# A two-layer encoder on one Trainium2 core: a weight sum of the first chunk moved to an accumulating transfer, more weight quarters kept live, two squares moved to VectorE

## Chip, cores, metric

The kernel runs on one core of one Trainium2 chip. The metric is the device time of one launch in microseconds; lower is better. Every stated time is that of the one core.

## The reference, cut to what matters

Two encoder layers over 512 tokens of width 1024. Each layer normalises `x`, multiplies it by one wide input matrix, runs a token mixer (dilated windows in layer 0, grouped queries in layer 1) and an attention over 256 memory tokens, gates the result and adds an output projection.

```python
def reference(x, mem, norm_g, mem_norm_g, w_mem_kv, mem_qn_g, mem_kn_g, w_out,
              w_in_a, qn_a, kn_a, w_in_b, qn_b, kn_b):
    ...
    for i in range(DEPTH):                       # 2 layers
        h = rmsnorm(x, norm_g[i])
        mem_h = rmsnorm(mem, mem_norm_g[i])
        j = i // 2
        if i % 2 == 0:
            proj = jnp.einsum('bsd,de->bse', h, w_in_a[j])   # 512 x 1024 x 11264
            ...
            o_mix = mixer_dilated(qkv, qn_a[j], kn_a[j], ang_a)
        else:
            proj = jnp.einsum('bsd,de->bse', h, w_in_b[j])
            ...
        o_mem = memory_attention(q_mem, mem_h, w_mem_kv[i], mem_qn_g[i], mem_kn_g[i])
        y = jnp.concatenate([o_mix, o_mem], axis=-1) * jax.nn.silu(gate)
        x = x + jnp.einsum('bse,ed->bsd', y, w_out[i])
    return x
```

All data are float32. The kernel keeps that accuracy by splitting each operand into a rounded high part and a remainder and multiplying three times.

## The kernel before

**Chunks.** The weights are cut on the host into pieces of 128x1024 (512 KB), and the program consumes them in chunks (`PLAN`, in the order `SEQ = [1, 2, 0, 3, 4, ...]`). Chunks 1 and 2 (kind `T2`) are the keys and values of the memory tokens in layer 0: plain products. Chunk 0 (`W2`) makes the values `v0`, chunk 3 (`W1`) the memory queries, chunks 4 and on the heads. These use seven quarter products in place of eight (the scheme of Winograd): the weight matrix is cut into the quarters `11`, `12`, `21`, `22`, and four weight sums are formed from them:

- `T1` = quarter `12` with quarter `11` added (the host writes the signs so that all are additions),
- `T2` = quarter `22` plus `T1`, `T3` = quarter `12` plus quarter `22`, `T4` = quarter `21` plus `T2`.

The products run in the order `21, 11, T1, T2, 22, T3, T4`. In a chunk of kind `W2` each consists of two pieces (x = 0 and 1), in `W1` of one.

**Steps.** Each group of matmuls on TensorE takes one weight piece for all its tokens; after it the program calls `W.advance()` (L335), which raises the step number `g` by one. Steps 0 to 3 are the memory keys, 4 to 7 the memory values, 8 to 21 chunk 0 (two steps for each product in the order above: 8 and 9 take `21`, 10 and 11 `11`, 12 and 13 `T1`, 14 and 15 `T2`, 16 and 17 `22`, 18 and 19 `T3`, 20 and 21 `T4`), 22 to 28 chunk 3, 29 and on chunk 4. What one step puts into the program comes in this order:

1. `lo()` (L314): VectorE makes the low part `wo` = piece minus `wh` of pieces whose high part was made in an earlier step (line L319).
2. `sum()` (L265): at most one weight sum, the first in the list of those still to be made whose conditions hold. The list holds `T1, T2, T3, T4` (x = 0, then 1) of each chunk in turn. `T1` of chunks below 17 is an addition on VectorE (L278), the others are accumulating transfers issued by GpSimd (`G.dma_start(..., accum_op=ALU.add)`): `T2` and `T4` from another tile (L283, L293), `T3` from DRAM (L288). The conditions are counted in steps: a piece that was loaded at least `LEAD` = 2 steps earlier (`ripe`) may be added to, and `T1` also waits for step `T1_AT` = 8.
3. `hi()` (L300): ScalarE rounds up to two pieces into `wh` (L309), in the order of the products.
4. `dma()` (L251): SyncE loads further pieces while fewer than `KEEP[kind]` of them are live (10 for `W2`, 9 for `W1` and the first heads), at most nine in one step. A piece is live from its load to its last use.

Then the driver's `tick()` runs the other work of that step (norms, evacuations, attention) as generators. The schedule is written out in this way: every engine and every DMA queue runs its instructions in the order in which the program was written, and an instruction waits, on its engine, for the semaphores of what it needs.

**The work around the change.** `prep()` (L961) normalises `x` in four blocks c = 0 to 3: `norm_1` (L480) squares both halves on ScalarE (L488) and forms the root on GpSimd (L490, then `rstd_of`, L448 and L449), `norm_2` multiplies (L495, VectorE), `first_t` and `diffs_t` transpose the blocks and form the differences of the token quarters (L552 to L562), `rest_t` the rest (L569 to L575). `mem_kv` makes the memory keys: squares per head (L594), the root on GpSimd (L448, L449), a rescale on GpSimd (L658), the multiplication `xn` on VectorE (L599), and a transposition `qT` on TensorE (L606). In `s_chunk` (L376) a finished product is copied out of its PSUM bank by ScalarE (`keep`, L384) or added by VectorE (`add`, L401). Four PSUM banks (`pj`) go round, so a product with a fresh bank waits for the copies of the one before. `v0` is stored to DRAM by SyncE (L1062) as it is finished.

Of the kernel before, what the change touches and what calls it, by code (L numbers as in the profile page):

```python
# [21 lines left out]
TCKW = {}  # L22
NBIG, NM4, NS2, SCRATCH = 7, 23, 14, 2048
RING, LEAD = 4, 2
BULK, ACTIVE, SET_AT, T1_AT, MEM_B, PREP_Y, PREP_B, HALF, SET_B = 2, 2, 15, 8, 14, 1, 1, {"a": 3, "b": 3, "o": 0}, 9
MEM_STEP = 1, 1
MEM_D = 4
DIRECT, DIRECT_B = (7,), (4, 5, 6, 7)
# [9 lines left out]

SEQ = [1, 2, 0] + list(range(3, len(PLAN)))
T4_AT = {4: 4}  # L40
T1_DMA = 17
KEEP = {"T2": 8, "T2b": 6, "O1": 6, "W1": 9, "W2": 10, "W2s": 9, "W1bs": 9, "W1b": 7, "W2b": 9}


# [84 lines left out]
def trunk_kernel(ctx: ExitStack, tc: tile.TileContext, x, mem, wall, norm_g, mem_norm_g, gcol,  # L129
# [59 lines left out]
    def pieces(kind):  # L189

        return 2 * GROUPS[kind][0] if kind in GROUPS else 4 if kind in ("W1", "W1b", "W1bs") else 8

    class Weights:
        def __init__(self):
            self.items, self.last, self.need, self.allocs, self.sums = [], [], [], [], []
            self.users, self.kinds = {}, []
            g = 0
            for c in SEQ:
                kind, d = PLAN[c], sum(pieces(k) for k in PLAN[:c])
                base = len(self.items)  # L200
                if kind in GROUPS:
                    units, nb = GROUPS[kind]
                    if kind == "O1":
                        n = PLAN[c - 1] == "O1"
                        for x in range(2):
                            self.items.append((c, "P", x))
                            self.last.append(g + 5)
                            self.allocs.append(((c, "P", x), d + x, kind))
                            self.users[c, "P", x] = 1
                        self.need += [base + 2] * 2 if not n else [base + 2] * 6  # L210
                        g += 2 if not n else 6
                        units = 0
                    for u in range(units):
                        for x in (2 * u, 2 * u + 1):
                            self.items.append((c, "P", x))
                            self.last.append(g + (u + 1) * nb - 1)
                            self.allocs.append(((c, "P", x), d, kind))
                            self.users[c, "P", x] = 1
                            d += 1
                        self.need += [base + 2 * u + 2] * nb  # L220
                    g += units * nb
                else:
                    n = 1 if kind in ("W1", "W1b", "W1bs") else 2
                    at = {k: d + i * n for i, k in enumerate(("21", "11", "12", "22"))}
                    self.allocs += [((c, k, x), at[q] + x, kind) for k, q in LOADS for x in range(n)]
                    for k in ORDER:
                        for x in range(n):
                            self.items.append((c, k, x))
                            self.last.append(g)
                            self.need.append(len(self.items))  # L230
                            if k[0] == "T":
                                self.sums.append(((c, k, x), at["11" if k == "T1" else "22"] + x))
                            if k != "T4":
                                self.users[c, k, x] = 1 if k in ("22", "T3") or k == "11" and c >= T1_DMA else 2
                            g += 1
                self.kinds += [kind] * (g - len(self.kinds))
            assert sum(pieces(k) for k in PLAN) == wall.shape[0]
            self.g = -1
            self.live = 0
            self.tile, self.load_at, self.at, self.lo_at = {}, {}, {}, {}  # L240
            self.n_hi = self.n_lo = self.taken = 0
            self.op, self.hi_at = [], []
# [6 lines left out]
                self.live -= 1  # L249

        def dma(self, most=9):  # L251
            while self.allocs and self.live < KEEP[self.allocs[0][2]] and most:
                most -= 1
                key, d, _ = self.allocs.pop(0)
                self.live += 1
                self.tile[key] = m4(name="wl")
                self.load_at[key] = self.g
                if key[1][0] != "T":
                    self.at[key] = self.g
                nc.sync.dma_start(self.tile[key], wall[d])  # L260
# [4 lines left out]
        def sum(self, force=False, want=None):  # L265

            for n, (key, d) in enumerate(self.sums[:8]):
                if want and key != want:
                    continue
                c, k, x = key  # L270
                if k == "T1" and c >= T1_DMA:
                    if not self.ripe(self.load_at, key, force):
                        continue
                    G.dma_start(self.tile[key], wall[d], accum_op=ALU.add)
                elif k == "T1":
                    if not (self.ripe(self.load_at, key, force) and self.ripe(self.at, (c, "11", x), force)) or self.g < T1_AT and not force:
                        continue
                    V.tensor_tensor(self.tile[key], self.tile[key], self.tile[c, "11", x], ALU.add)  # L278
                    self.use((c, "11", x))
                elif k == "T2":  # L280
                    if not (self.ripe(self.load_at, key, force) and self.ripe(self.at, (c, "T1", x), force, 1 if c < T1_DMA else None)):
                        continue
                    G.dma_start(self.tile[key], self.tile[c, "T1", x], accum_op=ALU.add)  # L283
                    self.use((c, "T1", x))
                elif k == "T3":
                    if not self.ripe(self.load_at, key, force):
                        continue
                    G.dma_start(self.tile[key], wall[d], accum_op=ALU.add)  # L288
                else:
                    if not (self.ripe(self.lo_at, (c, "21", x), force, 1) and self.ripe(self.at, (c, "T2", x), force, T4_AT.get(c))):  # L290
                        continue
                    self.tile[key] = self.tile[c, "21", x]
                    G.dma_start(self.tile[key], self.tile[c, "T2", x], accum_op=ALU.add)  # L293
                    self.use((c, "T2", x))
                self.at[key] = self.g
                self.sums.pop(n)
                return True
            return False

        def hi(self, force=False):  # L300
            i = self.n_hi
            if i >= len(self.items) or not self.ripe(self.at, self.items[i], force, 1 if self.items[i][1] == "T1" and self.items[i][0] < T1_DMA else None):
                return False
            if i >= RING and self.last[i - RING] > self.g - (not force and self.items[i - RING][1] != "P"):
                return False
            self.n_hi += 1
            wh = pool.tile([128, 1024], F32R, tag="wh", name="wh", bufs=RING)
            wo = pool.tile([128, 1024], F32R, tag="wo", name="wo", bufs=RING)
            A.copy(wh, self.tile[self.items[i]])  # L309
            self.hi_at.append(self.g)  # L310
            self.op.append((wh, wo))
            return True
# [167 lines left out]
    def norm_1(xb, both=False):  # L480

        ss = sm(2, "ss")
        for j in range(2):
            jk = s2(name="sq")
            if both and j:
                V.tensor_tensor_reduce(jk, xb[j], xb[j], 1.0 / 1024.0, 0.0, ALU.mult, ALU.add, ss[:, j:j + 1])
            else:
                A.activation(jk, xb[j], AF.Square, scale=1.0 / 32.0, accum_out=ss[:, j:j + 1])  # L488
        r, e = sm(1, "rstd"), sm(1, "mse")
        G.tensor_tensor(e, ss[:, 0:1], ss[:, 1:2], ALU.add)  # L490
        return rstd_of(e, 1)
# [463 lines left out]
    xb = [halves(t) for t in xt]  # L955

    def prep():

        n = {}
        for c in range(5):  # L960
            if c < 4:  # L961
                n[c] = norm_1(xb[c])
            if c:
                norm_2(xb[c - 1], n[c - 1], rows["x"])
            if 1 < c < 4:
                first_t(H, xb[c - 2], c - 2)
            yield 1
        for c in range(2):
            yield from diffs_t(H, xb[2 + c], c)
            drv.spawn(rest_t(H, c, (2, 2, 2)), 1)  # L970
            yield 1
# [689 lines left out]
```

## Time and profile before

| | |
|---|---|
| time, median of 3 runs | 956.48 us (955.04 to 957.57) |
| the profiled execution, its own time | 955.29 us |
| its span (first to last instruction) | 953.4 us |
| TensorE busy in the span | 939.3 us (99%) |
| VectorE, ScalarE, GpSimd busy | 790.3, 680.8, 336.0 us |
| mean granted TensorE clock | 0.998 |

How to read the profile: PE is TensorE, PEld its weight loads, DVE is VectorE, ACT is ScalarE, POOL is GpSimd, SP is SyncE; a q behind the name stands for the engine's sequencer, which issues transfers. `L278` is line 278 of the kernel before. A row of the timeline has start, duration, engine, line, operation, output <- input, the number of instructions merged into the row, and in brackets how long the engine had been idle before and what ended that. In the rows on transfers, q1 is the queue of SyncE's loads and stores, q0 that of GpSimd's accumulating transfers; both share 16 DMA engines.

### The profile page before, as it was taken

The numbers are of one execution on the slowest core, as the hardware profiler recorded it, in microseconds if no ns is written. First come the engines' busy times: TensorE is split into PE (matmuls) and PEld (weight loads), VectorE is DVE, ScalarE is ACT, GpSimd is POOL, SyncE is SP. The second block draws the span as 40 slices with busy tenths as digits, with TensorE's granted clock in tenths as the row PEclk, the third lists the DMA queues.
The fourth block names the chain that finished last, engine by engine and source line by source line (L and its number), as shares of the span: only waits on it lengthen the run. The fifth ranks groups of instructions, "written<-read, shape, count | busy, mean of one in ns | idle before, by whom it ended". The sixth has DMA issues, their size and how long they took to land.

```text
span 953.4 us, 16569 instructions
## 1 busy us (share of the span) xinstructions
PE 939.3 (99%) x5680; PEld 832.2 (87%) x5680; DVE 790.3 (83%) x1409; ACT 680.8 (71%) x1700; POOL 336.0 (35%) x484
## 2 busy tenths in 40 slices
PE   8999999999999999999999999999899999999998
PEld 6878888888888888888889998888899999998886
DVE  6878776878888888979788999877988898779982
ACT  7773789686868686767775768547778877878860
POOL 3312423557454546463836111213232330111110
PEclk9999999999999999999999999999999999999999
DMA  9699966869787869696877989979966687786524
GB/s 352 271 217 337 335 156 177 289 123 265 148 259 157 264 155 265 155 257 142 229 182 197 259 200 252 288 251 314 240 158 132 192 236 174 210 210 178 123 59 129
DMA packets 86198, 203.51 MB, mean 213 GB/s; under 512 B 25057, under 2 KB 34529, under 8 KB 86114
## 3 DMA queue, kind: packets, MB, share of 16 engines
q1 hardware_dynamic: 66962, 139.46, 42.8%
q0 software_dynamic: 17856, 60.83, 34.4%
q10 hardware_dynamic: 1296, 2.16, 0.6%
q8 instruction: 45, 0.74, 0.3%
q14 instruction: 39, 0.32, 0.1%
HBM read 156.48 MB, written 11.34 MB: 176 GB/s over the span
## 4 chain that ended last, share of the span: by engine, by line
PE 84%; DMA 6%; DVE 5%; ACT 3%; issue 1%; SPq 1%; POOL 0%; DVEq 0%; POOLq 0%; ACTq 0%
PE pj L173 22%; PE pj L174 22%; PE pj L177 22%; PE qT L606 2%; DMA wl<-in_wall_dram 2%; DMA wl<-wl 2%; DVE wo L319 2%; PE sa L1181 1%; PE oo L1289 1%; PE pt L1268 1%; PE ptb L1491 1%; PE sa L1177 1%; DMA x<-in_x_dram 1%; DMA row<-in_norm_g_dram 1%; PE ob L177 1%
## 5 line engine op out<-in xcount | busy, mean ns | idle before, releaser
L319 DVE TENSOR_TENSOR wo<-wl,wh 128x1024 fp32r<-128x1024 f32 x255 | 312.3, 1231 | 5.3 <-ACT wh L309 5.1
L309 ACT CAST wh<-wl 128x1024 fp32r<-128x1024 f32 x255 | 268.5, 1060 | 42.9 <-PE pj L174 18.9
L173 PE MATMUL pj<-wh,hS 128*128 128x512 f32 (+1 forms) x448 | 158.0, 366 | 4.5 <-ACT sn L384 3.7
L174 PE MATMUL pj<-wh,hS 128*128 128x512 f32 (+1 forms) x448 | 152.6, 354 | 0.6 <-DVE hS L570 0.6
L173 PE MATMUL pj<-wh,h 128*128 128x512 f32 (+1 forms) x336 | 118.0, 365 | 0.3 <-DVE sn L401 0.3
L174 PE MATMUL pj<-wh,h 128*128 128x512 f32 (+1 forms) x336 | 114.2, 353 | 1.1 <-DVE h L570 1.1
L449 POOL TENSOR_TENSOR rstd<-mse,half 128x4 f32<-128x4 f32 (+2 forms) x96 | 101.7, 1059 | 8.0
L177 PE MATMUL pj<-wo,hS 128*128 128x512 f32 (+1 forms) x448 | 100.7, 354 | 0.0
L173 PEld LDWEIGHTS pj<-wh,hS 128*128 128x128 f32 x448 | 85.1, 190 | 15.4 <-ACT sn L384 4.3
L174 PEld LDWEIGHTS pj<-wh,hS 128*128 128x128 f32 x448 | 85.2, 190 | 11.1 <-DVE hS L570 0.8
L177 PEld LDWEIGHTS pj<-wo,hS 128*128 128x128 f32 x448 | 75.3, 191 | 12.0
L448 POOL TENSOR_SCALAR mse<-hss 128x4 f32<-128x4 f32 (+1 forms) x86 | 41.2, 479 | 117.6 <-ACT junk L594 113.2
L594 ACT ACTIVATE junk<-sn 128x128 f32<-128x128 f32 x264 | 79.1, 308 | 1.3 <-DVE sn L395 1.2
L1125 POOL TENSOR_TENSOR ta<-sn,tabs 128x128 f32<-128x128 f32 (+1 forms) x64 | 37.6, 595 | 117.8 <-DVE sn L599 91.2
L384 ACT COPY sn<-pj 128x512 f32<-128x512 f32 x116 | 64.5, 590 | 17.4 <-PE pj L177 16.6
L177 PE MATMUL pj<-wo,h 128*128 128x512 f32 (+1 forms) x336 | 74.9, 352 | 0.0
L174 PEld LDWEIGHTS pj<-wh,h 128*128 128x128 f32 x336 | 63.7, 190 | 8.8 <-DVE h L570 1.3
L173 PEld LDWEIGHTS pj<-wh,h 128*128 128x128 f32 x336 | 63.6, 189 | 8.0 <-DVE sn L401 0.7
L293 POOL DMA_DIRECT2D wl<-wl x33 | 30.3, 918 | 109.1 <-DVE wo L319 59.8
L401 DVE TENSOR_TENSOR sn<-pj,sn 128x512 f32<-128x512 f32 x87 | 59.5, 685 | 7.7 <-PE pj L177 7.3
L177 PEld LDWEIGHTS pj<-wo,h 128*128 128x128 f32 x336 | 56.0, 189 | 8.8
L283 POOL DMA_DIRECT2D wl<-wl x33 | 31.3, 974 | 77.8 <-DVE grA L984 19.3
(250 smaller groups left out, 2365.2 us busy)
## 6 DMA issues: line engine op xcount, KB each, us to landing
wl<-in_wall_dram SPq DMA_DIRECT2D x222, 512.0 KB, 7.4
wl<-wl POOLq DMA_DIRECT2D x66, 512.0 KB, 5.4
wl<-in_wall_dram POOLq DMA_DIRECT2D x42, 512.0 KB, 8.9
od<-o SPq DMA_DIRECT2D x11, 256.0 KB, 5.5
og<-od SPq DMA_DIRECT2D x10, 256.0 KB, 8.2
x<-in_x_dram SPq DMA_DIRECT2D x4, 512.0 KB, 9.0
v0d<-sn SPq DMA_DIRECT2D x8, 256.0 KB, 10.2
acc<-in_x_dram POOLq DMA_DIRECT2D x8, 256.0 KB, 7.3
```

Source lines behind the costliest of these rows:

```text
L173: T.matmul(o, a, b, start=start, stop=False, skip_group_check=True)
L174: T.matmul(o, c, d, start=False, stop=False, skip_group_check=True)
L177: T.matmul(o, a, b, start=False, stop=stop, skip_group_check=True)
L283: G.dma_start(self.tile[key], self.tile[c, "T1", x], accum_op=ALU.add)
L309: A.copy(wh, self.tile[self.items[i]])
L319: V.tensor_tensor(wo, self.tile[key], wh.bitcast(F32), ALU.subtract)
L384: A.copy(t, b)
L401: V.tensor_tensor(t, b, t, ALU.subtract if q == "12" else ALU.add)
L448: G.tensor_scalar(e, ss, EPS, None, ALU.add)
L449: G.tensor_tensor(r, e, half[:, 0:n], ALU.pow)
L594: A.activation(jk, p[:, j * 128:(j + 1) * 128], AF.Square, scale=by, accum_out=ss[:, j:j + 1])
L1125: G.tensor_tensor(ta[:, 0:n], xn[:, 0:n, 0:32], ropeA[:, 0, b, s0:s0 + n], ALU.mult)
```

## The change

In chunk 0 the sum `T1` is no longer an addition on VectorE: GpSimd issues an accumulating transfer that adds quarter `11` from DRAM, from step 7 on (`T1_AT` now holds for the transfers only). The tile of quarter `11` then has one user instead of two. `KEEP_C` raises the number of live pieces at which loading stops, to 14 while pieces of chunk 0 or 3 are next and to 12 for chunk 4. In `prep()`, the second square of blocks 2 and 3 is made by VectorE.

```diff
-BULK, ACTIVE, SET_AT, T1_AT, ... = 2, 2, 15, 8, ...
+BULK, ACTIVE, SET_AT, T1_AT, ... = 2, 2, 15, 7, ...
...
-T1_DMA = 17
+T1_DMA = 0, 17
+KEEP_C = {0: 14, 3: 14, 4: 12}
...
+    def by_dma(c):
+
+        return c == T1_DMA[0] or c >= T1_DMA[1]
...
-                                self.users[c, k, x] = 1 if k in ("22", "T3") or k == "11" and c >= T1_DMA else 2
+                                self.users[c, k, x] = 1 if k in ("22", "T3") or k == "11" and by_dma(c) else 2
...
         def dma(self, most=9):
-            while self.allocs and self.live < KEEP[self.allocs[0][2]] and most:
+            while self.allocs and self.live < KEEP_C.get(self.allocs[0][0][0], KEEP[self.allocs[0][2]]) and most:
...
-                if k == "T1" and c >= T1_DMA:
-                    if not self.ripe(self.load_at, key, force):
+                if k == "T1" and by_dma(c):
+                    if not self.ripe(self.load_at, key, force) or self.g < T1_AT and not force:
                         continue
                     G.dma_start(self.tile[key], wall[d], accum_op=ALU.add)
                 elif k == "T1":
-                    if not (self.ripe(self.load_at, key, force) and self.ripe(self.at, (c, "11", x), force)) or self.g < T1_AT and not force:
+                    if not (self.ripe(self.load_at, key, force) and self.ripe(self.at, (c, "11", x), force)):
                         continue
                     V.tensor_tensor(self.tile[key], self.tile[key], self.tile[c, "11", x], ALU.add)
...
                 elif k == "T2":
-                    if not (... self.ripe(self.at, (c, "T1", x), force, 1 if c < T1_DMA else None)):
+                    if not (... self.ripe(self.at, (c, "T1", x), force, 1 if c < T1_DMA[1] else None)):
...
         def hi(self, force=False):
-            if ... not self.ripe(self.at, self.items[i], force, 1 if self.items[i][1] == "T1" and self.items[i][0] < T1_DMA else None):
+            if ... not self.ripe(self.at, self.items[i], force, 1 if self.items[i][1] == "T1" and not by_dma(self.items[i][0]) else None):
...
-                n[c] = norm_1(xb[c])
+                n[c] = norm_1(xb[c], c > 1)
```

With its second argument set, `norm_1` (L480) makes the second square by `V.tensor_tensor_reduce`.

More of the change, by code (lines that the diff above doesn't have):

```diff
@@ L24 @@
 RING, LEAD = 4, 2
-BULK, ACTIVE, SET_AT, T1_AT, MEM_B, PREP_Y, PREP_B, HALF, SET_B = 2, 2, 15, 8, 14, 1, 1, {"a": 3, "b": 3, "o": 0}, 9
+BULK, ACTIVE, SET_AT, T1_AT, MEM_B, PREP_Y, PREP_B, HALF, SET_B = 2, 2, 15, 7, 14, 1, 1, {"a": 3, "b": 3, "o": 0}, 9
 MEM_STEP = 1, 1
@@ L280, in sum @@
                 elif k == "T2":
-                    if not (self.ripe(self.load_at, key, force) and self.ripe(self.at, (c, "T1", x), force, 1 if c < T1_DMA else None)):
+                    if not (self.ripe(self.load_at, key, force) and self.ripe(self.at, (c, "T1", x), force, 1 if c < T1_DMA[1] else None)):
                         continue
@@ L301, in hi @@
             i = self.n_hi
-            if i >= len(self.items) or not self.ripe(self.at, self.items[i], force, 1 if self.items[i][1] == "T1" and self.items[i][0] < T1_DMA else None):
+            if i >= len(self.items) or not self.ripe(self.at, self.items[i], force, 1 if self.items[i][1] == "T1" and not by_dma(self.items[i][0]) else None):
                 return False
```

## The prediction

> **What bounds the kernel now.** I read the page first, then the table of busy time by stretches, then TensorE's waits, then the timeline of the first 110 us. The first two rows say that TensorE is the bound: 14.1 us of the span are without a matmul, of which 7.25 us lie in the first 200 us, where the change acts.
>
> ```profile
> PE 939.3 (99%) x5680; PEld 832.2 (87%) x5680; DVE 790.3 (83%) x1409; ACT 680.8 (71%) x1700; POOL 336.0 (35%) x484
> 0.00:200.00 200.00, 192.75 (x1009) 162.80 (x1010) 154.04 (x221) 144.25 (x353) 71.79 (x114) 0.99 0.85 263
> PE pj L173 <- ACT sn L384: 3.7, 2, 1.9
> 50.97 0.50 PE L173 MATMUL pj<-wh,hS 128*128 128x512 f32 x1 [1.90 <-ACT sn L384]
> 96.83 0.38 PE L173 MATMUL pj<-wh,hS 128*128 128x256 f32 x1 [1.78 <-ACT sn L384]
> ```
>
> Two stalls stand out: 1.90 us ahead of step 12 (the first product with `T1`) and 1.78 us in chunk 3. The first costs more than its length, because the granted clock (third number from the end in these rows) falls behind it:
>
> ```profile
> 52.00:53.00 1.00, 1.00 (x5) 0.80 (x4) 0.97 (x3) 0.94 (x3) 1.00 (x2) 0.71 1.06 188
> 53.00:54.00 1.00, 1.00 (x4) 0.81 (x3) 1.00 (x2) 1.00 (x2) 0.06 (x1) 0.50 1.08 127
> 54.00:55.00 1.00, 1.00 (x3) 0.76 (x3) 1.00 (x3) 1.00 (x3) 0.00 (x0) 0.50 0.97 184
> 55.00:56.00 1.00, 1.00 (x4) 0.79 (x3) 1.00 (x2) 1.00 (x3) 0.53 (x1) 0.58 1.06 205
> ```
>
> 0.29 + 0.50 + 0.50 + 0.42 = 1.7 us of full-speed work are lost there. So the change can win at most about 1.9 + 1.7 + 1.78 = 5.4 us at these places.
>
> **Part 1: two additions leave VectorE.** VectorE works almost without a pause from 33.2 to 51 us, and step 12 waits for the end of that: differences (L561), a cast and a copy on ScalarE, then TensorE.
>
> ```profile
> 33.19 0.69 DVE L599 TENSOR_TENSOR xn<-pj,rstd 128x512 f32<-128x512 f32 x1 [0.51 <-POOL rstd L658]
> 44.18 1.22 DVE L278 TENSOR_TENSOR wl<-wl 128x1024 f32<-128x1024 f32 x1
> 47.96 1.22 DVE L278 TENSOR_TENSOR wl<-wl 128x1024 f32<-128x1024 f32 x1
> 49.09 0.68 DVE L561 TENSOR_TENSOR fS<-xT,f 128x512 f32<-128x512 f32 x1
> ```
>
> From the second addition to the next start are 49.09 - 47.96 = 1.13 us, so both are worth 2.26 us on this chain, more than the stall of 1.90.
>
> **Part 2: two squares.** Each leaves ScalarE (0.64 + 0.20 us) and goes to VectorE. The operation exists before only at another width:
>
> ```profile
> L488 ACT ACTIVATE sq<-x x8: 622/636/652, 18.4 to 29.8; 128x512 f32<-128x512 f32 x8
> L1187 DVE CUSTOM_DVE_ANT_0 p<-sa,tabs 128x256 f32<-128x256 f32 x48 | 19.0, 421 | 1.2 <-PE sa L1177 1.0
> ```
>
> At 512 wide it lies between 0.42 (the fixed part only) and 0.84 us (twice); I take 0.7. Both stand ahead of L599, where VectorE idles 0.51 us for GpSimd; with that cover gone the second costs up to 0.3 us. I count it at nothing, since part 3 makes that idle time much longer.
>
> **Part 3: more live pieces, and what they pull forward.** Counting pieces by the code's rules: before, chunk 0 loads four pieces by step 4 beyond the first six, and its last two (for `T3`) at steps 8 and 9. With 14 allowed (and nine loads at most in a step) the two `T3` pieces are loaded at step 2. `sum()` takes the first sum whose conditions hold. `T1` is held until step 7 and `T2` needs `T1`, but `T3` needs only its own load, two steps old. So the two `T3` transfers, at steps 12 and 13 before, now enter GpSimd's queue at steps 4 and 5. At step 4 `sum()` comes ahead of `tick()`, which issues the root for block 3 of `x` and the rescale of the memory keys (L658). Before, those ran straight on:
>
> ```profile
> 30.34 1.39 POOL L449 TENSOR_TENSOR rstd<-mse,half 128x4 f32<-128x4 f32 x1
> 31.68 0.20 POOL L490 TENSOR_TENSOR mse<-ss 128x1 f32<-128x1 f32 x1
> 32.83 0.33 POOL L658 TENSOR_SCALAR rstd<-rstd,rm 128x4 f32<-128x4 f32 x1
> 45.73 1.08 POOL L283 DMA_DIRECT2D wl<-wl  x1 [12.57 <-DVE wl L278]
> ```
>
> The first `T3` transfer will stand between the first two of these rows and wait there for its piece to land. That piece is the eleventh load of the weights after `x`, before and after: the first of these three issues.
>
> ```profile
> 29.12 2.87 SPq L260 DMA_DIRECT2D wl<-in_wall_dram  x3
> wl<-in_wall_dram SPq DMA_DIRECT2D x1, 512.0 KB, 10.2
> q1 hardware_dynamic: 228, 0.83, 103.7%
> q1 hardware_dynamic: 11, 0.03, 4.1%
> ```
>
> It landed at 29.1 + 10.2 = 39.3 us. An earlier issue doesn't bring it forward: the last two rows (36 to 38 us, 40 to 42 us) show the DMA engines full with such loads up to 38 us and empty after 40; they drain a queue whose order is unchanged. GpSimd does hold everything behind such a wait:
>
> ```profile
> 107.93 0.18 ACT L594 ACTIVATION_READ_ACCUMULATOR junk<-sn 128x1 f32 x1
> 108.80 0.92 POOL L293 DMA_DIRECT2D wl<-wl  x1 [3.42 <-DVE wo L319]
> 109.80 0.22 POOL L448 TENSOR_SCALAR mse<-hss 128x4 f32<-128x4 f32 x1
> ```
>
> The sum at 109.80 had its squares at 108.11 and began only after the transfer ahead of it was released and issued, 1.0 us after 108.80.
>
> So: 39.3 + 1.0 (issue) + 1.5 (31.68 to 33.16) = 41.8 us for the end of L658, against 33.2. `xn` (L599) runs 41.8 to 42.5, and TensorE, in order, stands at its transposition:
>
> ```profile
> 36.64 0.60 PE L606 MATMUL qT<-ident,xn 128*128 128x128 f32 x4
> 36.99 0.48 PE L173 MATMUL pj<-wh,h 128*128 128x512 f32 x1
> 48.00 1.07 PE L177 MATMUL pj<-wo,h 128*128 128x512 f32 x4
> ```
>
> That is a new stall of 42.5 - 36.6 = 5.9 us, with a clock loss behind it that I take from the rows above at 1.7 us (half to one and a half times that, by where the gap falls). TensorE then ends step 11 at 42.5 + (49.07 - 36.64) + 1.7 = 56.6. VectorE's chain is 41.8 - 33.2 = 8.6 us late and 2.26 us shorter: step 12 starts at 50.97 + 6.35 = 57.3. The old stall shrinks to 0.7 us, too short to be followed by the old clock loss: **+6.35 - 1.7 = +4.6 us** by the end of chunk 0's `T1` products.
>
> **Part 4: when the `T1` transfers land.** Two bounds for an accumulating transfer: alone, and against a full queue of loads.
>
> ```profile
> wl<-wl POOLq DMA_DIRECT2D x1, 512.0 KB, 4.8
> wl<-wl POOLq DMA_DIRECT2D x1, 512.0 KB, 9.3
> q0 software_dynamic: 86, 0.29, 73.6%
> q1 hardware_dynamic: 86, 0.22, 31.6%
> ```
>
> The first was issued at 45.73 (row above), alone, the second at 75.67 (row in part 5); the last two rows (82 to 84 us) show both queues at work: 0.29 MB in 2 us is 3.6 us for 512 KB. `T1` stands behind both `T3`. Against loads (18 rather than 13 now precede the first store of `v0` on SyncE) the first `T3` lands at 39.3 + 9.3 = 48.6, the first `T1` at 48.6 + 2 x 3.6 = 55.8. ScalarE must have rounded it (1.05 us) before the cast at 56.1, or hold that cast and the copy for step 12: 0.8 us late. Alone, everything is in time. I take the full queue, as the six loads of chunk 3 now follow at once: **+0.8**. The second `T1` at 59.4 is rounded by 60.5, in time for step 13 at 60.8.
> The Trainium skill (DMA: Bandwidth & Descriptors, "Queues, rings and completion order") says that a DMA engine goes round its queues packet by packet. The 86 and 86 packets agree. But even if all 4.8 us of the lone transfer were stretched by the 73.6% that q0 gets, that makes 6.5 us and not 9.3. By the rule alone `T1` would be in time and the sum 0.8 lower.
>
> **Part 5: chunk 3.** The second stall ends a chain of late loads:
>
> ```profile
> 66.01 9.13 DMA wl<-in_wall_dram
> 75.67 9.34 DMA wl<-wl
> 85.60 8.41 DMA wl<-wl
> 94.09 1.05 ACT wh L309
> 96.31 0.48 ACT sn L384
> ```
>
> Its pieces now load at steps 4 to 11 instead of 11 to 16, ahead of the blocking store, so the load at 66 and the transfer at 75.7 move forward by over 10 us and the stall goes: **-1.78**. The additions of chunk 4 move up from steps 24 and 25 to 20 and 22 on VectorE (below).
>
> Sum: 4.6 + 0.8 - 1.8 = **+3.6, say +3.7 us**: 955.29 + 3.7 = 959.0 for a profiled execution, which lay 1.2 below the median of the runs; for the median 956.48 + 3.7 = **960.2 us**. By itself this case spans 957.8 (short clock loss, `T1` in time) to 963.5. About 0.3%, 2.9 us, is what a measurement tells from no change.
>
> **Rivals.**
> *Faster, at 951.* The mechanism is the one place on which the rest depends: if the wait at step 4 held nothing, because the `T3` piece lands by 31.7 us, all of 1.9 + 1.7 + 1.78 would be won. Against it stand the full DMA engines up to 38 us and the waiting row at 108.80. It decides at a landing before about 34 us. Chance 0.13.
> *No difference, 957 to 959.3.* The same stall, but a landing some 2 us earlier or a clock that recovers at once (-1.7), with `T1` in time (-0.8): +1 to +2.8. Chance 0.22.
> *Slower still, by a wait on VectorE, at 962 to 965.* Chunk 4's first addition, before:
>
> ```profile
> 90.61 1.23 DVE L278 TENSOR_TENSOR wl<-wl 128x1024 f32<-128x1024 f32 x1 [1.34 <-DMA wl<-in_wall_dram]
> ```
>
> It now precedes the low part of chunk 3's quarter `11`. If its load landed no earlier than 90.6, that low part would be done at about 93, over 2 us later than step 23 wants it, with the clock loss on top. The load moves up four steps, which speaks against it. Chance 0.13. A second way there: `T1` late by 2 us more, so that step 12 waits 2.8 us and the clock falls again. By the row at 50.97 (1.90 us, half clock) that costs another 1.7 us; by the row at 96.83 (1.78 us) not.
> The Trainium skill (TensorE: Matmul & The Clock Gate, "HAM oscillation — how this bites in real kernels") puts the limit at gaps of about 3.4 us. The 1.90 us gap disagrees; by the page that case would be 1.7 us shorter. Chance 0.07.
> *The loads don't come earlier* (SyncE waits for buffers): the stall of part 3 stays or shrinks with the landing, the 1.78 us stay lost: about 962. Chance 0.05.
>
> **Numbers.** Forecast 0.40; faster 0.13; same 0.22 and slower 0.65 with the rest. The range 955.8 to 965.2 leaves out the faster case and a little at the top.
>
> **What would show it.** Right: a GpSimd transfer from DRAM at about 39 us between L449 and L490; TensorE idle 5 to 6 us before `qT`, ended by VectorE's `xn`; half clock behind it; no addition at 44 and 48 us; no wait at chunk 3's copy. Wrong: the root of block 3 still at 32 us, or the stall present and the total unchanged or lower, which would mean that I mis-sized what parts 1 and 5 give back.

## The result, and the profile after

| | before | after |
|---|---|---|
| median, runs side by side | 957.07 us (955.04 to 958.60, 11 runs) | 959.20 us (957.93 to 960.96, 11 runs) |
| the profiled execution, its own time | 955.29 us | 958.25 us |
| its span | 953.4 us | 956.5 us |

The ratio is 1.0022, with a 95% interval of 1.0012 to 1.0032: slower, by 1 to 3 us. The medians differ by 2.1 us, the profiled executions by 2.96 us, their spans by 3.1. In the program after, the lines that are spoken of have moved by 5 (L599 is L604, L278 is L283, L288 is L293 and so on); in `keep_only` they moved by 1.

The page's row of TensorE, the row of the first 200 us (same columns as before) and the one long stall in the timeline of TensorE:

```profile
PE 940.2 (98%) x5680; PEld 833.1 (87%) x5680; DVE 788.8 (82%) x1411; ACT 679.6 (71%) x1696; POOL 339.3 (35%) x486
0.00:200.00 200.00, 190.51 (x989) 160.88 (x990) 151.22 (x223) 140.71 (x338) 72.94 (x113) 0.98 0.87 265
42.80 1.09 PE L611 MATMUL qT<-ident,xn 128*128 128x128 f32 x4 [6.04 <-DVE xn L604]
```

TensorE lost 2.24 us more in the first 200 us. The stalls of 1.90, 0.27 and 1.78 us are gone, one of 6.04 us has come. The chain of waits, in order of time, shows where it starts: two DMA pieces of 10 and 11 us, a transfer on GpSimd, the transposition.

```profile
17.40 10.22 DMA wl<-in_wall_dram
27.69 11.00 DMA wl<-in_wall_dram
39.34 1.07 POOL wl L293
42.80 1.09 PE qT L611 x4
```

GpSimd's timeline has the place. The root of block 3 (L495) stood at 31.68 before; now a transfer that waits for its piece stands between it and L454:

```profile
29.67 1.33 POOL L454 TENSOR_TENSOR rstd<-mse,half 128x4 f32<-128x4 f32 x1
39.34 1.07 POOL L293 DMA_DIRECT2D wl<-in_wall_dram  x1 [8.34 <-DMA wl<-in_wall_dram]
40.18 0.47 POOL L495 TENSOR_TENSOR mse<-ss 128x1 f32<-128x1 f32 x1
...
41.62 0.30 POOL L663 TENSOR_SCALAR rstd<-rstd,rm 128x4 f32<-128x4 f32 x1
41.87 0.92 POOL L293 DMA_DIRECT2D wl<-in_wall_dram  x1
42.52 2.07 POOL L279 DMA_DIRECT2D wl<-in_wall_dram  x2
53.07 0.86 POOL L288 DMA_DIRECT2D wl<-wl  x1 [8.48 <-DMA wl<-in_wall_dram]
56.85 0.86 POOL L288 DMA_DIRECT2D wl<-wl  x1 [2.93 <-DMA wl<-in_wall_dram]
```

The rows at 53.07 and 56.85 are the `T2` transfers, and each waits for its `T1`: so the two `T1` transfers, issued from 42.52 on, had landed by 53.07 and 56.85. The granted clock behind the stall (third number from the end), by stretches of 1 us:

```profile
41.00:42.00 1.00, 0.00 (x0) 0.00 (x0) 0.04 (x1) 0.00 (x0) 0.95 (x3) 0.93 1.07 410
42.00:43.00 1.00, 0.20 (x1) 0.23 (x2) 1.00 (x2) 0.00 (x0) 1.00 (x2) 0.50 1.08 254
...
47.00:48.00 1.00, 1.00 (x4) 0.71 (x4) 1.00 (x2) 0.00 (x0) 0.00 (x0) 0.50 1.07 205
48.00:49.00 1.00, 1.00 (x6) 0.75 (x5) 0.91 (x3) 0.81 (x2) 0.00 (x0) 0.66 1.05 266
```

TensorE works at half clock from 42.8 to past 48: 0.1 + 5 x 0.5 + 0.34 = 2.9 us of full-speed work lost. The balance is 6.04 + 2.9 - 1.90 - 1.7 - 1.78 - 0.27 = +3.3 us, against 3.1 in the spans.

SyncE's wait, its next loads, and the transfers from 44 to 48 us:

```profile
SPq L265 <- DVE x L500: 9.1, 1, 9.1
44.00 1.68 SPq L265 DMA_DIRECT2D wl<-in_wall_dram  x3
q0 software_dynamic: 229, 0.81, 104.1%
q1 hardware_dynamic: 2, 0.01, 0.5%
```

SyncE itself waited 9.1 us, up to 44.0, for the multiplication of block 3 (L500), which the same stall had held up and which ended at 43.98. Then it issued three loads within 1.7 us, but from 44 to 48 us nearly none of their data moved: the accumulating transfers, whose issue began before theirs, had the DMA engines to themselves. The wait explains why no load was issued up to 44.0. That the three loads then stood back up to about 48 is what the rows show; the reason isn't shown.

VectorE's timeline has the two squares, 0.69 us each, and chunk 4's first addition, which now waits:

```profile
22.53 0.69 DVE L491 CUSTOM_DVE_ANT_0 sq<-x 128x512 f32<-128x512 f32 x1
29.41 0.69 DVE L491 CUSTOM_DVE_ANT_0 sq<-x 128x512 f32<-128x512 f32 x1
85.32 1.23 DVE L283 TENSOR_TENSOR wl<-wl 128x1024 f32<-128x1024 f32 x1 [2.05 <-DMA wl<-in_wall_dram]
```

### The profile page after: what moved, and what is told of

Read it like the earlier page. It is cut to its first block, busy times and chain, and to the rows that moved or that the text cites. A ratio compares the mean times of both kernels' runs of the same rounds, so it can differ in the third digit from the quotient of the medians.

```text
span 956.5 us, 16572 instructions
## 1 busy us (share of the span) xinstructions
PE 940.2 (98%) x5680; PEld 833.1 (87%) x5680; DVE 788.8 (82%) x1411; ACT 679.6 (71%) x1696; POOL 339.3 (35%) x486
## 3 DMA queue, kind: packets, MB, share of 16 engines
q10 hardware_dynamic: 1296, 2.16, 0.6%
## 4 chain that ended last, share of the span: by engine, by line
PE 89%; DMA 4%; DVE 3%; ACT 2%; issue 1%; POOL 1%; SPq 0%; DVEq 0%; POOLq 0%; ACTq 0%
PE pj L175 23%; PE pj L174 23%; PE pj L178 23%; PE qT L611 2%; DMA wl<-in_wall_dram 2%; PE sa L1186 1%; PE oo L1294 1%; PE pt L1273 1%; PE ptb L1496 1%; PE sa L1182 1%; DVE wo L324 1%; DMA x<-in_x_dram 1%; PE ob L178 1%; PE ob L175 1%; PE ob L174 1%
## 5 line engine op out<-in xcount | busy, mean ns | idle before, releaser
L324 DVE TENSOR_TENSOR wo<-wl,wh 128x1024 fp32r<-128x1024 f32 x255 | 315.7, 1244 | 6.0 <-ACT wh L314 5.7
L314 ACT CAST wh<-wl 128x1024 fp32r<-128x1024 f32 x255 | 268.6, 1060 | 33.3 <-PE pj L175 19.2
L454 POOL TENSOR_TENSOR rstd<-mse,half 128x4 f32<-128x4 f32 (+2 forms) x96 | 101.3, 1056 | 8.0
L453 POOL TENSOR_SCALAR mse<-hss 128x4 f32<-128x4 f32 (+1 forms) x86 | 43.2, 503 | 112.1 <-ACT junk L599 107.8
L599 ACT ACTIVATE junk<-sn 128x128 f32<-128x128 f32 x264 | 79.1, 308 | 2.2 <-DVE sn L400 2.2
L1130 POOL TENSOR_TENSOR ta<-sn,tabs 128x128 f32<-128x128 f32 (+1 forms) x64 | 35.4, 561 | 118.2 <-DVE sn L604 91.2
L288 POOL DMA_DIRECT2D wl<-wl x33 | 30.9, 960 | 66.3 <-DMA wl<-in_wall_dram 11.4
```

Source lines behind the costliest of these rows:

```text
L324: V.tensor_tensor(wo, self.tile[key], wh.bitcast(F32), ALU.subtract)
L453: G.tensor_scalar(e, ss, EPS, None, ALU.add)
L454: G.tensor_tensor(r, e, half[:, 0:n], ALU.pow)
L599: A.activation(jk, p[:, j * 128:(j + 1) * 128], AF.Square, scale=by, accum_out=ss[:, j:j + 1])
L1130: G.tensor_tensor(ta[:, 0:n], xn[:, 0:n, 0:32], ropeA[:, 0, b, s0:s0 + n], ALU.mult)
```

## The experiments

All diffs are against the program after unless said otherwise. Theory W at the start: the wait at step 4, which the raised limit of chunk 0 brings, is what costs; the `T1` transfers gain. Rivals: the raised limits cost in other ways too (the queues), or `T1` by transfer gains nothing.

**1. The three parts, one at a time.** `T1` by transfer alone:

```diff
-KEEP_C.get(self.allocs[0][0][0], KEEP[...])
+KEEP[self.allocs[0][2]]
-n[c] = norm_1(xb[c], c > 1)
+n[c] = norm_1(xb[c])
```

> The kernel before with the first part of the change alone: T1 of chunk 0 by accumulating transfers from step 7 on; live pieces and squares as before. Theory: T3 is loaded at step 8, so nothing stands at steps 4 and 5; the two additions leave VectorE, the 1.90 us stall at step 12 and the 1.7 us of clock behind it go, the 1.78 us stall in chunk 3 stays: 3 to 3.6 us below before, about 953.5. Rival (the extra accumulating transfers are the cost): no gain or a loss, 957 or more, with a wait for T1 ahead of step 12.

Measured: 950.71 us (949.83 to 951.59), ratio 0.9939 [0.9925, 0.9952]. That is better than expected, because chunk 3's stall has gone too, though no limit was raised. Three rows of its timeline (GpSimd, ScalarE, TensorE; here `wl L283` is still chunk 3's own addition `T1`):

```profile
67.44 0.88 POOL L288 DMA_DIRECT2D wl<-wl  x1 [13.30 <-DVE wl L283]
87.83 1.05 ACT L314 CAST wh<-wl 128x1024 fp32r<-128x1024 f32 x1 [1.74 <-DMA wl<-wl]
94.47 0.66 PE L1096 MATMUL qT<-ident,sn 128*128 128x128 f32 x4 [0.37 <-DVE sn L604]
```

The transfer of chunk 3's `T2` stood at 75.67 before and stands at 67.44 now, the rounding at 94.09 stands at 87.83. Of the old stall 0.37 us are left elsewhere: 1.90 + 1.7 + 1.78 + 0.27 - 0.37 = 5.3 us, the difference of the spans (953.4 - 948.1).

Why chunk 3's stall went shows in SyncE's loads, two rows of before and two of this run:

```profile
58.73 2.49 SPq L260 DMA_DIRECT2D wl<-in_wall_dram  x2
66.01 6.33 SPq L260 DMA_DIRECT2D wl<-in_wall_dram  x6
...
29.23 3.77 SPq L265 DMA_DIRECT2D wl<-in_wall_dram  x4
56.33 2.48 SPq L265 DMA_DIRECT2D wl<-in_wall_dram  x2
```

The row at 29.23 has four loads; the one at 29.12 in the prediction's part 3 has three. The fourth, at 32.66, is quarter `11` of chunk 3, which before was the first of the two at 58.73, behind the store of `v0`. The piece for chunk 3's `T2` then comes second at 56.33 (it is issued at 57.59), ahead of the four small loads of the tables, where before it stood behind them at 66.01. So loads did come earlier. By the code's rules that is due to `T1_AT` = 7 instead of 8: each sum of chunk 0 stands one step earlier and its tiles come free one step earlier, so that quarter `11` of chunk 3 loads at step 13 instead of 14. No run changes this step alone; by the same count it would move these loads as much with the additions left on VectorE. How the 5.3 us divide between the transfer and the earlier step is therefore not shown.

The raised limits alone (before, with only this):

```diff
+KEEP_C = {0: 14, 3: 14, 4: 12}
-while self.allocs and self.live < KEEP[self.allocs[0][2]] and most:
+while self.allocs and self.live < KEEP_C.get(self.allocs[0][0][0], KEEP[...]) and most:
```

> The kernel before with the second part of the change alone: 14, 14 and 12 live pieces for chunks 0, 3 and 4; T1 stays two additions on VectorE. Theory: T3 stands at steps 4 and 5, so the stall ahead of qT and its half clock are there as in the changed kernel (6.0 and 2.8 us), and VectorE's additions make step 12 another 2 us later (at about 59.7), while the stall in chunk 3 is gone: 5 to 7 us above before, 962 to 964. Rival (more live pieces are the good part of the change and the transfers for T1 the bad one): 1.5 us or more below before.

Measured: 962.20 us (961.80 to 962.73), ratio 1.0059 [1.0045, 1.0073], as expected. TensorE's stalls:

```profile
43.29 1.09 PE L607 MATMUL qT<-ident,xn 128*128 128x128 f32 x4 [6.39 <-DVE xn L600]
60.22 0.50 PE L174 MATMUL pj<-wh,hS 128*128 128x512 f32 x1 [2.16 <-ACT sn L385]
```

The squares alone (before, with `norm_1(xb[c], c > 1)`):

> The kernel before with the two squares on VectorE alone. Theory A (hidden): 956.2 to 957.4, ratio 0.9995 to 1.0005, TensorE's stalls as before (1.90 at step 12, 1.78 in chunk 3). Rival (0.7 us of VectorE ahead of xn, and the chain to step 12 is VectorE's): up to 0.7 us more at step 12, with 1.7 us more of half clock: up to 958.5.

Measured: 956.56 us (954.64 to 960.97), ratio 0.9989 [0.9976, 1.0002]: no difference that these runs can tell. And the squares with `T1` by transfer, that is `KEEP_C = {}`:

> The change without its raised limits on live pieces: the T1 transfers and the two squares stay. T1 by transfer alone gave 950.7 us. Theory A (the squares are off the path: xn waits for GpSimd's rstd anyway): 950 to 951.5, ratio to before 0.993 to 0.9955, no TensorE stall before 165 us longer than 0.3 us but the one at the start. Rival (the second square stands ahead of xn on VectorE and takes up to 0.3 us more than the idle time there): 951.0 to 951.5, with a new stall of up to 0.3 us at qT.

Measured: 951.34 us (950.13 to 951.50), ratio 0.9933 [0.9919, 0.9946], the same as `T1` alone. The one new stall, 0.63 us at 8.18, lies ahead of the squares.

**2. Which limit.** With `KEEP_C = {0: 14}`:

> The change with its limit for chunk 0 alone; chunks 3 and 4 back at the old ones. The T3 transfers stand at steps 4 and 5 of GpSimd, chunk 3's pieces load from step 11. Theory W (the wait at step 4 costs its stall and the clock behind it, whatever chunks 3 and 4 do): a stall of 5.5 to 6.5 us at qT, 951.3 + 6.0 + 2.8 = 958.5 to 961; the table loads land in about 8 us. Rival (chunk 0's limit is harmless by itself and chunk 3's pieces cost): 951 to 953.

Measured: 959.33 us, ratio 1.0018 [1.0007, 1.0030]; the stall is there:

```profile
42.77 1.08 PE L611 MATMUL qT<-ident,xn 128*128 128x128 f32 x4 [6.25 <-DVE xn L604]
```

With `KEEP_C = {3: 14, 4: 12}`:

> The change with its limits for chunks 3 and 4 but chunk 0 back at its old one: the T3 pieces of chunk 0 load at step 8 and their transfers stand at steps 11 and 12; chunk 3's pieces load from step 8, chunk 4's from step 14. No wait stands ahead of block 3's root, so qT must have no stall. Theory A (only the wait at step 4 costs): 950 to 951.5, as without any raised limit. Theory B (loads pulled forward also cost, by filling the queue ahead of small loads and accumulating transfers): 953 to 957, with the small table loads (grA) landing over 12 us after their issue instead of 8.1 and VectorE waiting for them at its scale, the copy sn and TensorE behind it.

Measured: 958.68 us, ratio 1.0013 [1.0002, 1.0024]. So theory W, as the whole cause, has fallen: nothing waits at step 4 and yet 7 us of the gain are gone. The stall stands elsewhere (timeline of VectorE and TensorE):

```profile
77.01 0.21 DVE L989 TENSOR_SCALAR grA<-grA 128x96 f32<-128x96 f32 x1 [7.14 <-DMA grA<-in_qn_a_dram]
77.87 0.79 PE L174 MATMUL pj<-wh,h 128*128 128x512 f32 x1 [5.00 <-DVE sn L406]
```

VectorE waits at a product of 0.2 us for a 48 KB table, and the addition `sn` for which TensorE waits is the next instruction behind it. The tile's rows on transfers, from issue to landing, in this run and in `T1` alone:

```profile
DMA to landing us min/median/max: 16.9/18.7/20.5
...
DMA to landing us min/median/max: 8.1/8.1/8.1
```

**3. The wait at step 4 taken away, all limits kept.** `T3` held until `T1` has gone (steps 11 and 12):

```diff
-if not self.ripe(self.load_at, key, force):
+if not self.ripe(self.load_at, key, force) or c == 0 and self.g < T1_AT and not force:
```

> The changed kernel with one condition more: the two T3 transfers of chunk 0 are held until step 7 as well, so that they enter GpSimd's queue at steps 11 and 12, behind the norms. Theory (the wait of the first T3 transfer on GpSimd holds the root of block 3 and the rescale of the memory keys, and that alone makes the change a loss): the 6.0 us stall ahead of qT and the half clock behind it (2.8 us) go, the two old stalls stay away; 5 to 6 us below the kernel before, about 951.5. If chunk 4's addition on VectorE then has to wait for its load (85.3 us in the changed kernel), up to 2 us of that are lost again. Rival (the extra traffic of the accumulating transfers and of the earlier loads is the cost): it stays at the changed kernel's 959, since all of that traffic is still there.

Measured: 957.97 us (956.56 to 958.50), ratio 1.0011 [1.0001, 1.0020], not 951.5. The stall at `qT` is gone, but the table's has come (rows of VectorE and TensorE), with 0.79 us more at 60.56:

```profile
76.88 0.21 DVE L989 TENSOR_SCALAR grA<-grA 128x96 f32<-128x96 f32 x1 [6.34 <-DMA grA<-in_qn_a_dram]
77.75 0.79 PE L174 MATMUL pj<-wh,h 128*128 128x512 f32 x1 [4.18 <-DVE sn L406]
```

`T3` only one step later, behind the root and the rescale (`or c == 0 and self.g < 5`):

> The change with one thing different: the first T3 transfer of chunk 0 may not go before step 5, so that it stands behind block 3's root and the rescale on GpSimd (steps 5 and 6 instead of 4 and 5). Same loads in the same order. Theory A (it is the place in GpSimd's queue, not the loads, that makes the 6.0 us stall): no stall at qT, xn at about 33.2, span shorter by the stall and the 2.8 us of clock behind it, 950 to 952 if nothing else is late. Theory B (loads pulled forward also cost): qT stall gone too, but new stalls by late transfers or small loads take back 2 to 5 us: 953 to 957. Rival C (the stall comes from the loads themselves): stall at qT stays, 958 to 960.

Measured: 960.36 us (959.08 to 962.31), ratio 1.0033 [1.0021, 1.0046], a time near rival C's, but without its stall at `qT`, and above the figures of A and B. GpSimd, ScalarE and TensorE:

```profile
41.09 2.05 POOL L293 DMA_DIRECT2D wl<-in_wall_dram  x2 [7.08 <-DMA wl<-in_wall_dram]
42.82 2.10 POOL L279 DMA_DIRECT2D wl<-in_wall_dram  x2
56.91 1.04 ACT L314 CAST wh<-wl 128x1024 fp32r<-128x1024 f32 x1 [9.88 <-DMA wl<-in_wall_dram]
59.01 0.80 PE L174 MATMUL pj<-wh,hS 128*128 128x512 f32 x1 [8.74 <-ACT sn L389]
```

The `T1` transfers stand behind the waiting `T3`, are issued at 42.8 instead of 33.3 (in the run before this one), and the first lands at 56.9. Step 12 pays 8.74 us. In the program after, where loads had been held, `T1` had landed by 53.07, and TensorE came to step 12 only at 57.81: there it didn't show.

`T3`'s pieces loaded third and fourth, the transfers held to steps 4 and 5, where the program after has them:

```diff
-for k, q in LOADS for x in range(n)
+for k, q in (LOADS if c else LOADS[:1] + LOADS[5:] + LOADS[1:5]) for x in range(n)
...
-if not self.ripe(self.load_at, key, force):
+if not self.ripe(self.load_at, key, force) or c == 0 and self.g < 4 and not force:
```

> The changed kernel with the pieces for T3 of chunk 0 loaded third and fourth instead of eleventh and twelfth; the T3 transfers stay at steps 4 and 5 in GpSimd's queue. Theory (it is the landing of the piece that counts, not the place of the transfer as such): the piece lands at about 29 us, before GpSimd gets there at 31, so the transfer is issued without a wait and costs about 1 us on GpSimd; total 951 to 954. A second theory (a transfer from DRAM at that place holds GpSimd whatever it waits for, or its traffic takes the bandwidth from the loads): a stall of several us stays ahead of qT, total 956 to 959.

Measured: 956.40 us (955.67 to 957.28), ratio 0.9997 [0.9988, 1.0007], not the gain. The transfer stands at 31.59 without a wait, and again `T1` follows two transfers: stalls of 0.83, 0.87 and, for `T2`, 1.82 us:

```profile
31.59 1.08 POOL L293 DMA_DIRECT2D wl<-in_wall_dram  x1
59.30 0.51 PE L174 MATMUL pj<-wh,hS 128*128 128x512 f32 x1 [1.82 <-ACT wh L314]
```

**4. The order in the load queue.** `T3` held as in `gate_t3`, and the tables issued six steps earlier, used where they were:

```diff
-BULK, ACTIVE, SET_AT, ... = 2, 2, 15, ...
+BULK, ACTIVE, SET_AT, ... = 2, 2, 9, ...
-        yield 4
+        yield 10
```

> The run with T3 held back (gate_t3), and beside that the four small table loads (mask, tabA, two parts of grA) issued at step 8 instead of step 14; VectorE and GpSimd use them at the same steps as before (18 to 20). Without this edit grA landed 19.7 us after its issue, VectorE stood 6.34 us at grA and TensorE 4.18 us behind it. Theory Q (the small loads' place in the load queue makes that stall): no wait of VectorE for grA and no stall at 77 us; 957.97 - 4.18 - about 2.5 of clock - something of the 0.79 stall left: 950.5 to 952.5. Rival (the DMA engines are simply too full with the raised limits, whatever the order): another late transfer takes the place, 954 to 958.

Measured: 957.52 us (955.65 to 960.09), ratio 1.0009 [0.9998, 1.0021]. The table's stall is gone; issued at 41.7 instead of 57.1, the table took even longer to land (22 to 26 us) but was in time. The time is the rival's, by a new stall:

```profile
85.08 1.23 DVE L283 TENSOR_TENSOR wl<-wl 128x1024 f32<-128x1024 f32 x1 [8.95 <-DMA wl<-in_wall_dram]
87.50 2.08 PE L178 MATMUL pj<-wo,h 128*128 128x256 f32 x8 [5.69 <-DVE wo L324]
```

This is chunk 4's first addition, standing on VectorE ahead of a low part that TensorE needs. So the same with chunk 4's limit taken back, `KEEP_C = {0: 14, 3: 14}`:

> The run before (T3 held back, small tables loaded at step 8) with chunk 4's limit back at its old value; chunks 0 and 3 keep 14. There chunk 4's first addition stood at step 22 on VectorE and waited 8.95 us for a load that landed only at 85.08, and TensorE waited 5.69 us behind it; now it stands at step 24, two steps later, and chunk 4's loads start at step 17 instead of 14. Theory Q (each raised limit puts something in the load queue ahead of what is needed next; without chunk 4's the last stall goes): no wait of that addition that TensorE sees, 957.5 - 5.7 - 2.5 of clock + 0: 949.5 to 951.5, that is no better than T1 by transfer alone (950.7). Rival (the transfers are late by themselves as soon as the queue is full): yet another stall of over 1 us before 100 us, 953 to 957.

Measured: 950.36 us (948.92 to 951.49), ratio 0.9927 [0.9910, 0.9944]: theory Q. The addition still waits 3.06 us, at 87.19, but two steps later in the order, and TensorE has no stall over 0.3 us between the start and 130 us. The DMA engines were no less busy for it; the rows of what they moved from 36 to 84 us, first of `tables_early`, then of this run:

```profile
DMA packets 4937, 14.02 MB, mean 292 GB/s; under 512 B 1246, under 2 KB 1374, under 8 KB 4933
...
DMA packets 5206, 14.17 MB, mean 295 GB/s; under 512 B 1282, under 2 KB 1410, under 8 KB 5201
```

So the two runs don't differ in how full the engines are, but in what stands ahead of what. And the same with the tables back at step 14:

> The last run (950.36) with the four small table loads back at step 14: T3 held back, limits raised for chunks 0 and 3 only. It tells which of the two edits carried that result. Theory Q (the tables' place in the load queue matters by itself): grA lands over 15 us after its issue, VectorE waits for it 4 to 7 us at about 76 us, TensorE stalls 2 to 5 us behind it, with about 2.5 of clock: 955 to 958. Rival (it was chunk 4's limit alone; without it the queue is short enough for the tables at step 14 as well): no stall, 949.5 to 951.5.

Measured: 956.67 us, ratio 0.9991 [0.9976, 1.0005]: the table's stall is back.

```profile
77.24 0.21 DVE L989 TENSOR_SCALAR grA<-grA 128x96 f32<-128x96 f32 x1 [6.89 <-DMA grA<-in_qn_a_dram]
78.10 0.79 PE L174 MATMUL pj<-wh,h 128*128 128x512 f32 x1 [4.76 <-DVE sn L406]
```

One of its 12 runs, not the profiled one, took 950.29; what was in time there the runs don't show. With `T3` held, the four cases are:

| | chunk 4's limit 12 | chunk 4's limit as before |
|---|---|---|
| tables at step 14 | 957.97 | 956.67 |
| tables at step 8 | 957.52 | 950.36 |

The spans fit the stalls to within 1.2 us. Beyond the 948.2 us of `KEEP_C = {}`, whose own two stalls that the others lack are 0.63 (at 8.18) and 0.47 us (at 94.60):

| run | stalls + clock loss - 1.10 | span more |
|---|---|---|
| after | 6.04 + 2.9 - 1.10 = 7.8 | 8.3 |
| `t3_step5` | 8.74 + 0.85 + 2.8 - 1.10 = 11.3 | 12.3 |
| `gate_t3` | 4.18 + 0.79 + 1.4 - 1.10 = 5.3 | 6.5 |
| `t1_sq_late_keep` | 5.00 + 0.83 + 2.4 - 1.10 = 7.1 | 7.5 |
| `tables_early` | 5.69 + 0.31 + 2.8 - 1.10 = 7.7 | 8.0 |
| `gate_keep03` | 4.76 + 0.78 + 2.7 - 1.10 = 7.1 | 8.0 |
| `t1_sq_keep0` | 6.25 + 0.34 + 2.6 - 1.10 = 8.1 | 8.0 |
| `t3_loaded_early` | 1.82 + 0.87 + 0.83 + 0.32 + 0.32 + 1.7 - 1.10 = 4.8 | 6.0 |

## Why the prediction came out, and where it was wrong

The forecast was +3.7 us. The profiled executions differ by 3.0 us, the medians by 2.1 us, less than forecast. By its size alone the result also lies in the range of the rival "No difference" (957 to 959.3). Of that rival's conditions one held, `T1` in time; the clock did not recover at once, and the piece landed at 27.69 + 11.00 = 38.7 us, 0.6 us ahead of the forecast and not 2. So the stall, its place and what released it are the forecast's, and the size is in part luck, as part 4 shows.

**Part 1** holds. The two additions are gone, and `t1_only`, which also has the earlier step, shows the stall and its clock loss gone with them.

**Part 2** holds: 0.69 us each, worth nothing that two comparisons can tell.

**Part 3**, the stall, holds nearly to the tenth: the rescale ended at 41.92 (forecast 41.8), TensorE stood 6.04 us (5.9), and the first `T3` transfer stood where it was put. The term that was mis-sized is the clock loss: 2.9 us, not 1.7. It was taken from the row behind a 1.90 us gap, where half clock lasted 3.4 us; behind the 6 us gap it lasted 6.8 us, and TensorE worked in 5.9 of them. Of the 1.2 us more, 0.7 went into the 0.7 us stall that the forecast still had ahead of step 12, where none was measured; step 12 came at 57.81 instead of 57.3, 0.5 us late.

**Part 4** failed in the program after: no stall at step 12, so +0.8 was wrong. I took the full queue. Next to no loads moved just then: SyncE was held 9.1 us by the same stall, and the three loads that it issued from 44.0 on stood back up to about 48. The even share of the row for 82 to 84 us (86 packets each) isn't general, since from 44 to 48 us the two queues had 229 and 2. The price itself was about right: in `t3_step5`, where SyncE wasn't held, the first `T1` landed at 56.9 (55.8 forecast). The two errors at step 12, 0.5 us too low by the clock and 0.8 us too high here, nearly cancelled: that is luck. The shift at step 12, 57.81 - 50.97 = 6.84 us, less 1.7, 1.78 and 0.27 gives the +3.1 us of the spans.

**Part 5** has the right amount, and an earlier load is what takes the stall away, but raised limits aren't needed for it. The piece that was loaded at 66.01 is loaded at 44.00 in the program after and at 57.59 in `t1_only`, which wins the 1.78 us with the old limits. The transfer behind it moved from 75.67 to 69.16 in the program after, 6.5 us and not over 10. The raised limits bring nothing that the runs can show: the best run with any of them, 0.9927 [0.9910, 0.9944], can't be told from `T1` alone, 0.9939 [0.9925, 0.9952].

**The faster rival** called the wait at step 4 "the one place on which the rest depends". This is the step of the reasoning that failed most. Seven runs raise limits and have no wait at that place; six of them take 956.4 to 960.4 us, not 951. Behind the wait lay three more, which came out one after another as the one ahead was taken away: `T1` behind `T3` on GpSimd, the tables behind the pieces on SyncE, chunk 4's addition ahead of a low part on VectorE. The last is the third rival's mechanism: in the program after it waited 2.05 us at no cost, in `tables_early` it set the end.

Still open: why a 48 KB table takes 6 to 10 us from issue to landing in eight of the 14 kernels (8.6 in before and after), 11 to 13 in `t3_loaded_early` and 17 to 26 in the other five. Only its place in the program was varied, not its size or its queue. Open, too, is what `T1_AT` = 7 is worth without the transfer.

## What to carry to other kernels

A deeper prefetch is an edit to every queue that it passes through: list, for each engine, what each early transfer or addition now stands ahead of, and whether that can wait for the data. When a wait is removed and the time doesn't move, look for the next one in the same trace before giving up the part that gains; here one of three edits (the transfers with their earlier step) was worth 6 us and another took it back. Price a stall with the clock behind it, from a stall of its own length.

## What the hardware showed unexpectedly

An accumulating transfer occupies the DMA engines about twice as long as a load of the same bytes: alone it moved 0.81 MB in 4 us at 104% (row above); loads alone moved as much in 2 us (36 to 38 us of the program after):

```profile
q1 hardware_dynamic: 220, 0.81, 101.5%
```

For 512 KB that makes 2.6 and 1.3 us, worked out from the two rows.

Whether a gap of about 2 us costs the clock isn't told by its length in these runs. Behind the 1.82 us of `t3_loaded_early` the clock fell, behind the 2.16 us of `keep_only` it didn't (1 us stretches, in that order):

```profile
62.00:63.00 1.00, 1.00 (x4) 0.81 (x3) 0.00 (x0) 1.00 (x2) 0.53 (x1) 0.50 1.14 406
...
61.00:62.00 1.00, 1.00 (x6) 0.80 (x5) 1.00 (x2) 1.00 (x2) 0.00 (x0) 1.00 1.04 197
```

The gap of 1.82 us had another of 0.87 us ahead of it, 3 us earlier. But `squares_only` shows the same without such a neighbour: half clock (0.50 from 52 to 54 us) behind its gap of 1.83 us at 50.71, none behind its gap of 2.34 us at 97.17.

The Trainium skill (TensorE: Matmul & The Clock Gate, "HAM oscillation — how this bites in real kernels") gives about 3.4 us of idle time as the limit. All gaps longer than that which these profiles show (4.18 to 8.74 us) were followed by half clock, which agrees; the 1.82 us of this fence and the 1.90 us of before, also followed by it, do not.
